# Second and third FFN: seven half-size products from the seventh unit on, and an adding transfer for the weights used last

## The chip, the cores and the metric

The kernel runs on one core of one Trainium2 chip. A core has TensorE (PE in the profile; its weight loads are shown apart as PEld), VectorE (DVE), ScalarE (ACT), GpSimd (POOL) and SyncE (SP), each with an instruction stream of its own, worked off in order, and 16 DMA engines that all queues share. The metric is the device time in microseconds of one execution; the median over several runs counts.

## The reference

The reference is a small diffusion transformer of two layers over 256 latent tokens and 256 context tokens, width 1024, in float32. Each layer has half an FFN, a mixer (attention in the first, an mLSTM in the second) and half an FFN again, each with a modulation by the condition `c` before and a normalised residual sum behind it. Cut to what matters here:

```python
def half_ffn(h, shift, scale, gate, w_in, w_out, g, b):
    xm = modulate(h, shift, scale)            # h * (1 + scale) + shift
    a, u = jnp.split(xm @ w_in, 2, axis=-1)   # 1024 -> 2 x 2816
    y = (jax.nn.silu(a) * u) @ w_out          # 2816 -> 1024
    return post_norm(h, 0.5 * gate * y, g, b)

# per layer i: mod_lat = silu(c) @ ada_w[i] + ada_b[i], cut into nine vectors (shift, scale, gate
# of three parts); mod_ctx likewise from c_ctx
# order: FFN (0,0), attention, FFN (0,1), FFN (1,0), mLSTM, FFN (1,1); the last for latents alone
```

The first three FFNs work on latents and context together, 512 tokens.

## The kernel before

**Numbers in two parts.** TensorE multiplies in a rounded 32-bit format (fp32r). To keep float32's accuracy every operand x is held as h (x rounded) and l = x - h, and every product is three matmuls, h·h, h·l, l·h (`mm3`, line 238). The parts are made by `split` (lines 222 and 227): a copy on ScalarE gives h, a subtraction on VectorE gives l. Activations lie as `xh` and `xl`, 128 partitions x 8 blocks x 512 tokens (the latents' 256 first, `LAT`, then the context's, `CTX`).

**Weights.** A chunk is 128 x 1024 floats, 512 KB. `raw` loads it from SyncE's queue (line 207) into one of `RAW` = 3 buffers; `pair` takes one of `WB` = 7 buffers for its h and l; `split` fills them.

**An FFN** (`ffn`) has 22 units of 128 hidden columns, in two halves of 11, since the hidden values of one half (`gt`) fit in memory: 11 units, then eight output products over those 11 (`unit_out`), twice. An ordinary unit (`unit_in`) takes two chunks and 16 blocks of weights, 48 matmuls of 512 columns, into two PSUM tiles, and `ffn_g` (lines 568, 569) forms silu(a)·u and splits it. The first four units of an FFN (`LEAD`) run on the latents first and on the context later, while the norm before them is still ending for the context. At the end of the second half the last four output products run by latents and context apart, with the steps of the next norm in between.

**The fast units.** In the second half of the second and third FFN, `fast_in` treats the unit's product as a 2 x 2 block product (two halves of the depth; latents and context; a and u) and forms it from seven half-size products instead of eight, after Strassen and Winograd: 84 matmuls of 256 columns. It needs sums of weight blocks, made on VectorE for each unit (`s1` to `s4`, line 615, into a tile of their own), and sums of activations, made once in `fast_sums` during the last output products of the first half: three new operands (`made`), and the lower context half of `xh`, `xl` overwritten. Line 650 is the unit's SiLU, lines 649, 653 and 654 its other VectorE steps.

**Modulation vectors.** They are made by VectorE: `ada_load` (line 331) brings 128 rows of the weight matrix, 512 KB, and `ada_dot` (line 337) multiplies them with the silu of c or c_ctx (`cb`) and sums, a dot. What layer 1 needs (40 loads for both vectors, 32 for one, 112 dots) is spread over the second and third FFN by the table `DOTS`: so many dots behind every unit (`in`) and output product (`out`). A load and its dots are written one directly behind the other; two buffers. `cb` is loaded and put through silu again (`silu_all`, line 306) whenever the memory has been used by the fast units.

**What sets the order.** The kernel is written on a tile framework: a planner at build time simulates the engines and issues, for each, what is ready by its own clock, earlier written first; buffers and waits follow from that. The chip then runs each stream in exactly that order. An instruction given to `pin` stays behind the one written before it on its engine: the dots, the norm's small steps and the residual steps (`residual`, lines 543 and 544: the old residual is scaled, two blocks behind every ordinary unit) are pinned. So a VectorE instruction that waits for a load holds up all behind it.

## Time and profile before

| | |
|---|---|
| median of 3 runs | 1652.38 us (1650.39 to 1652.40) |
| the profiled execution | 1649.32 us, span 1647.6 us |
| TensorE busy | 1617.8 us, 98% |
| VectorE busy | 1353.8 us, 82% |
| ScalarE busy | 744.2 us, 45% |
| read from memory | 249.81 MB, 152 GB/s over the span |
| mean granted TensorE clock | 0.993 |

The span goes from the first to the last instruction. By the times of the SiLUs, the second FFN runs from about 577 to 930 us of the span and the third to about 1300; the mLSTM follows to about 1457, the last FFN to the end. A line of a group reads: code line, engine, operation, output<-inputs, shapes, count | busy time, mean ns of one | idle time of the engine just before them and what ended it. A stage's line reads: from:to, length, then the busy time of PE, PEld, DVE, ACT and POOL with the number of instructions, the granted clock, the DMA engines' busy share and GB/s. Matmuls overlap in the engine, so the distance of their starts, not their length, says what one costs.

### The profile page before, as it was taken

How to read it: one execution, taken by the hardware profiler on the slowest of the kernel's cores; microseconds unless marked ns; L12 is line 12 of the kernel's file. 1: busy time of each engine (PE TensorE's matmuls, PEld its weight loads, DVE VectorE, ACT ScalarE, POOL GpSimd, SP SyncE). 2: the span in 40 equal slices, each digit the busy share in tenths (PEclk: the TensorE clock that was granted, in tenths of full speed). 3: DMA queues.
4: the chain of work that ended last, by engine and by line, in shares of the span. 5: the costliest groups of instructions: out<-in, count | busy, mean ns of one | idle time of the engine just before them, and what ended most of it. 6: DMA issues, size and time to landing. Idle time of an engine off the chain costs nothing. (4 is left out here: it accounts for less than half of the span.)

```text
span 1647.6 us, 26587 instructions
## 1 busy us (share of the span) xinstructions
PE 1617.8 (98%) x10308; PEld 1457.4 (88%) x10308; DVE 1353.8 (82%) x2689; ACT 744.2 (45%) x1269; POOL 61.6 (4%) x76
## 2 busy tenths in 40 slices
PE   9999999999999999999999999899999999999998
PEld 6888888899988998889999998689999989999987
DVE  5899978649888879999977977799965968897687
ACT  5532222314676343425652433225652656656542
POOL 0000000001011200000000100000000100020000
PEclk9999999999999999999999999899999999999999
DMA  9577765622103247733353267733352342437652
GB/s 371 187 237 231 239 215 187 203 76 84 65 1 91 64 143 229 229 128 129 103 182 126 78 193 255 250 120 116 115 155 66 116 120 78 135 109 256 181 172 96
DMA packets 72495, 252.59 MB, mean 153 GB/s; under 512 B 7984, under 2 KB 10800, under 8 KB 72368
## 3 DMA queue, kind: packets, MB, share of 16 engines
q1 hardware_dynamic: 71792, 250.10, 47.8%
q8 instruction: 81, 1.33, 0.3%
q10 hardware_dynamic: 576, 0.79, 0.1%
q14 instruction: 46, 0.38, 0.1%
HBM read 249.81 MB, written 1.05 MB: 152 GB/s over the span
## 5 line engine op out<-in xcount | busy, mean ns | idle before, releaser
L238 PE MATMUL t<-t,t 128*128 128x256 f32 (+2 forms) x8412 | 1325.1, 319 | 14.2 <-ACT t L222 10.7
L238 PEld LDWEIGHTS t<-t,t 128*128 128x128 f32 x8412 | 1193.1, 189 | 133.9 <-ACT t L222 12.7
L222 ACT CAST t<-t 128x1024 fp32r<-128x1024 f32 (+3 forms) x521 | 429.6, 844 | 467.3 <-PE t L238 244.3
L227 DVE TENSOR_TENSOR t<-t,t 128x256 fp32r<-128x256 f32 (+2 forms) x740 | 514.7, 728 | 116.6 <-ACT t L222 112.5
L337 DVE SCALAR_TENSOR_TENSOR t<-t,t 128x1024 bf16<-128x1024 f32 x224 | 263.5, 1220 | 25.2 <-DMA t<-in_ada_w 24.5
L909 PE MATMUL t<-t,t 128*128 128x256 f32 (+1 forms) x256 | 79.5, 311 | 0.0
L911 PE MATMUL t<-t,t 128*128 128x256 f32 (+1 forms) x256 | 78.8, 308 | 0.0
L910 PE MATMUL t<-t,t 128*128 128x256 f32 (+1 forms) x256 | 78.4, 306 | 0.0
L568 ACT ACTIVATE t<-t 128x512 f32<-128x512 f32 (+1 forms) x71 | 34.3, 487 | 95.6 <-PE t L238 95.6
L692 DVE SCALAR_TENSOR_TENSOR t<-t,t,t 128x256 f32<-128x256 f32 x96 | 42.7, 478 | 37.0 <-PE t L238 37.0
L569 DVE TENSOR_TENSOR t<-t,t 128x512 f32<-128x512 f32 (+1 forms) x71 | 38.9, 551 | 32.8 <-PE t L238 26.7
L464 POOL TENSOR_TENSOR t<-t,t 128x256 f32<-128x256 f32 x30 | 23.4, 781 | 1130.9 <-ACT t L454 1129.7
L1424 PE MATMUL t<-t,t 128*128 128x512 f32 (+3 forms) x286 | 60.2, 365 | 2.0 <-ACT t L1501 1.0
L837 PE MATMUL t<-t,t 128*128 128x512 f32 (+1 forms) x300 | 60.7, 364 | 0.0
L1424 PEld LDWEIGHTS t<-t,t 128*128 128x128 f32 (+2 forms) x286 | 43.8, 159 | 18.3 <-issue 2.2
L837 PEld LDWEIGHTS t<-t,t 128*128 128x128 f32 x300 | 51.4, 189 | 9.1 <-DVE t L831 0.3
L454 ACT ACTIVATE t<-t 128x256 f32<-128x256 f32 x72 | 26.2, 411 | 72.3 <-DVE t L447 72.3
L544 ACT ACTIVATE t<-t,t 128x256 f32<-128x256 f32 x64 | 29.4, 503 | 57.4 <-DVE t L543 57.4
L909 PEld LDWEIGHTS t<-t,t 128*128 128x128 f32 x256 | 48.4, 189 | 2.7
L910 PEld LDWEIGHTS t<-t,t 128*128 128x128 f32 x256 | 48.2, 188 | 2.6
L911 PEld LDWEIGHTS t<-t,t 128*128 128x128 f32 x256 | 48.1, 188 | 2.5
L615 DVE TENSOR_TENSOR t<-t,t 128x512 f32<-128x512 f32 x66 | 45.3, 686 | 1.1 <-DMA t<-in_ffn_in 0.3
(200 smaller groups left out, 1065.5 us busy)
## 6 DMA issues: line engine op xcount, KB each, us to landing
t<-in_ffn_in SPq DMA_DIRECT2D x168, 512.0 KB, 4.1
t<-in_ada_w SPq DMA_DIRECT2D x137, 512.0 KB, 4.2
t<-in_ffn_out SPq DMA_DIRECT2D x66, 512.0 KB, 4.4
t<-in_ffn_last SPq DMA_DIRECT2D x22, 512.0 KB, 3.5
t<-in_att_in SPq DMA_DIRECT2D x12, 512.0 KB, 3.5
t<-in_c SPq DMA_DIRECT2D x8, 512.0 KB, 7.8
t<-in_att_out SPq DMA_DIRECT2D x8, 512.0 KB, 3.5
t<-in_ml_qk SPq DMA_DIRECT2D x8, 512.0 KB, 3.6
```

Of the source, the lines that this page charges most:

```text
L222: self.behind(self.nc.scalar.copy(h, x))
L227: self.behind(self.nc.vector.tensor_tensor(out=ls, in0=xs, in1=hs.bitcast(F32), op=ALU.subtract))
L238: mm = lambda *k, **kw: self.nc.tensor.matmul(*k, skip_group_check=not group, **kw)
L337: ins = nc.vector.scalar_tensor_tensor(self.tmp().bitcast(BF16), r, 1.0, self.cb[:, v, :], ALU.mult, ALU.mult, accum_out=to)
L569: V.tensor_tensor(out=sl, in0=sl, in1=pu[:, :n], op=ALU.mult)
L615: add = lambda o, x, y: V.tensor_tensor(out=o, in0=x, in1=y, op=ALU.add)
L692: V.scalar_tensor_tensor(z, y[:, gg[0] - t0 : gg[1] - t0], gate()[:, v, d : d + 1], z, ALU.mult, ALU.add)
L837: pin(nc.tensor.matmul(o, gs[g], ws[k][w][:, i : i + n], start=k == k0 and g == w == 0, stop=k == k1 - 1 and g == 1,))
L909: mm(o, self.xh[:, k, c], wh, start=k == 0, stop=False)
L910: mm(o, self.xh[:, k, c], wl, start=False, stop=False)
L911: mm(o, self.xl[:, k, c], wh, start=False, stop=k == ND - 1)
L1424: mm = lambda *k, **kw: pin(nc.tensor.matmul(*k, **kw))
```

## The change

Three things are changed together, all for the second and third FFN, with what they need around them.

- From the seventh unit on (`FIRST` = 6) units are fast, in both halves: 16 of 22 for 11. So the sums of activations are made in the lead units: `fast_sums` behind the second lead unit's context part, in whole pieces of 1024 columns, and `fast_last`, which overwrites the lower context half, behind the last ordinary unit's matmuls. The buffers of `gt` for units 7 to 10 lend their room to these sums before they are needed (`gtiles`).
- In a fast unit the sums of weights are made in place in the two raw chunks, in another order, and the products come in the order a11, s1, s2, s4, s3, a12, a22. The pair of a12 and a22, used last, gets its parts by `split_added`: ScalarE writes h and -h, and a transfer from GpSimd's queue reads the chunk from memory a second time and adds it to -h.
- The dots: a load is issued at one call and its dots are made at a later one (`ada`, `flush`); `DOTS` names units one by one, and has places in the mLSTM too; counted through the loop `some`, the second FFN makes 46 dots, the third 47, the mLSTM 19 (there were 68, 44 and none). `cb` is loaded once and stays. One ada buffer while the fast units' operands are in memory and in the mLSTM.

Memory moves with it: a fourth raw buffer, five buffers for temporaries (a sixth where an FFN, the attention or the last FFN has room), the norm's sums in a pool of their own.

```diff
...
-RAW = 3
+RAW = 4
...
-SUMSAT = 4
+FIRST = 6
+GONE = 7
 FLIP = 56
 DOTS = {
-    1: {("in",): 4, ("out", 0): 3, ("out", 1): 2},
-    2: {("in",): 3, ("out", 0): 2, ("out", 1): 3},
+    1: {**{("in", j): 2 for j in (6, 8, 10, 12, 15, 18, 21)}, **{("out", 0, d): 2 for d in range(6)},
+        ("out", 0, 6): 4, ("out", 0, 7): 4, **{("out", 1, d): 2 for d in range(3)}, ("out", 1, 3): 4},
+    2: {**{("in", j): 2 for j in (6, 8, 10, 12, 15, 18, 21)}, **{("out", 0, d): 2 for d in range(6)},
+        ("out", 0, 6): 4, ("out", 0, 7): 4, **{("out", 1, d): 2 for d in range(3)}, ("out", 1, 3): 4},
+    "ml": {**{("key", n): 1 for n in range(5)}, **{("val", n): 1 for n in range(6)}, **{("unit", n): 1 for n in range(9)}, ("unit", 9): 2, ("unit", 10): 2},
 }
...
         self.fine = False
 
         self.nraw, self.spare = 0, None
+        self.ntmp, self.extra = 0, None
...
     def tmp(self, w=512):
-        return self.t([P, 512], tag="tmp", bufs=6)[:, :w]
+        self.ntmp += 1
+        if self.extra and self.ntmp % 6 == 0:
+            return self.t([P, 512], tag="tmpx", bufs=1, pool=self.extra)[:, :w]
+        return self.t([P, 512], tag="tmp", bufs=5)[:, :w]
...
+    def split_added(self, x, h, l, src=None):
+        self.nc.scalar.copy(h, x)
+        self.nc.scalar.activation(l, x, AF.Copy, scale=-1.0)
+        self.nc.gpsimd.dma_start(l, x if src is None else src, accum_op=ALU.add)
...
+        self.cb = self.t([P, 2, D])
+        self.waiting = []
+        self.norms(2)
+
...
+    def norms(self, n):
+        self.npool, self.np = self.right()
+        self.adas = self.np, n
...
-        r = self.t([P, 1024], tag="ada", bufs=2, pool=self.cp)
+        pool, n = self.adas
+        r = self.t([P, 1024], tag="ada", bufs=n, pool=pool)
...
     def ada(self, layer, dt, vecs=(0, 1)):
-        r = self.ada_load(layer, dt)
-        for v in vecs:
-            self.ada_dot(r, layer, dt, v)
+        self.waiting.append((self.ada_load(layer, dt), layer, dt, vecs))
+
+    def flush(self, n=0):
+
+        done = 0
+        while len(self.waiting) > n:
+            r, layer, dt, vecs = self.waiting.pop(0)
+            for v in vecs:
+                self.ada_dot(r, layer, dt, v)
+            done += len(vecs)
+        return done
...
+    def gtiles(self, j):
+        if j not in self.gt:
+            n, i = self.gw, j % NFH - GONE
+            if self.gn == NF or i < 0:
+                bufs = NF if self.gn == NF else GONE
+                self.gt[j] = tuple(self.t([P, n], F32R, tag=k, bufs=bufs, pool=self.gp) for k in ("gh", "gl"))
+            else:
+                assert i % 2 == 0
+                x = self.t([P, 4 * n], F32R, tag=f"g{i}", bufs=1, pool=self.gp)
+                for m in range(2):
+                    self.gt[j + m] = tuple(x[:, (2 * m + k) * n : (2 * m + k + 1) * n] for k in range(2))
+        return self.gt[j]
...
-    def fast_sums(self, i):
+        at = [i * n + (FLIP if i > 3 else 0) for i in range(6)]
+        self.slots = [x[:, a : a + n].rearrange("p (k f) -> p k f", f=TL) for a in at]
+        self.made = [self.slots[i : i + 2] for i in (0, 2, 4)]
+
+    def fast_sums(self):
 
...
+        lo, up = slice(0, ND // 2), slice(ND // 2, ND)
+        k = lambda x, i: x[:, i * 1024 : (i + 1) * 1024].rearrange("p (k f) -> p k f", f=TL)
+        x2, x1 = (self.t([P, 2048], tag=f"g{i}", bufs=1, pool=self.gp) for i in (0, 2))
+        t3, t2, t1, t4 = k(x2, 0), k(x2, 1), k(x1, 0), k(x1, 1)
+        add = lambda o, x, y, op=ALU.add: V.tensor_tensor(out=o, in0=x, in1=y, op=op)
+        less = lambda o, x, y: V.scalar_tensor_tensor(o, x, -1.0, y, ALU.mult, ALU.subtract)
+
+        def whole(o, ks, g):
+            add(o, self.xh[:, ks, g[0] : g[1]].bitcast(F32), self.xl[:, ks, g[0] : g[1]].bitcast(F32))
+
+        whole(t1, lo, LAT)
+        whole(t3, lo, CTX)
+        add(t1, t1, t3, ALU.subtract)
+        whole(t4, up, CTX)
+        add(t3, t4, t3, ALU.subtract)
+        less(t2, t1, t4)
+        whole(t4, up, LAT)
+        less(t4, t2, t4)
+        self.split(t3, *self.made[1])
+        self.split(t2, *self.made[0])
+        self.kept = t1, t4
+
+    def fast_last(self):
+
+        t1, t4 = self.kept
+        self.split(t1, *(x[:, : ND // 2, TL:T] for x in (self.xh, self.xl)))
+        self.split(t4, *self.made[2])
+
+    def fast_in(self, j, w_in):
...
         r0, r1 = (self.raw(w_in[2 * j + i]) for i in range(2))
-        sums = self.t([P, 4 * half], tag="sums", bufs=1, pool=st)
         part = lambda x, i: x[:, i * half : (i + 1) * half]
-        a11, a21, a12, a22 = part(r0, 0), part(r0, 1), part(r1, 0), part(r1, 1)
-        s1, s2, s4, s3 = (part(sums, i) for i in range(4))
-        add = lambda o, x, y: V.tensor_tensor(out=o, in0=x, in1=y, op=ALU.add)
-        ws = [self.pair(sh=SH, n=half)] + [self.pair(sh=SH) for _ in range(3)]
-        self.split(a11, *ws[0])
-        self.split(r1, *ws[1])
-        add(s1, a21, a22)
-        add(s2, s1, a11)
-        self.split(sums[:, : 2 * half], *ws[2])
-        add(s4, s2, a12)
-        add(s3, a11, a21)
-        self.split(sums[:, 2 * half :], *ws[3])
-        w = {n: [part(x, i) for x in ws[p]] for n, p, i in (
-            ("a11", 0, 0), ("a12", 1, 0), ("a22", 1, 1), ("s1", 2, 0), ("s2", 2, 1), ("s4", 3, 0), ("s3", 3, 1),
+        (a11, a21), (a12, a22) = ([part(r, i) for i in range(2)] for r in (r0, r1))
+        w1, w0, w2, w3 = self.pair(sh=SH), self.pair(sh=SH), self.pair(sh=SH, n=half), self.pair(sh=SH)
+        add = lambda o, x: V.tensor_tensor(out=o, in0=o, in1=x, op=ALU.add)
+        self.split_added(r1, *w1, w_in[2 * j + 1])
+        add(a22, a21)
+        add(a21, a11)
+        self.split(r0, *w0)
+        add(a11, a22)
+        add(a12, a11)
+        self.split(a11, *w2)
+        self.split(r1, *w3)
+        w = {n: [part(x, i) for x in p] for n, p, i in (
+            ("a11", w0, 0), ("s3", w0, 1), ("a12", w1, 0), ("a22", w1, 1), ("s2", w2, 0), ("s4", w3, 0), ("s1", w3, 1),
         )}
...
         a, u = self.tmp(), self.tmp()
         product(x, "a11", of(0, LAT), True, False)
         S.copy(a[:, :TL], x)
-        product(y, "a12", of(ND // 2, LAT), True, True)
         product(v, "s1", of(0, CTX), True, False)
         S.copy(u[:, TL:], v)
         product(x, "s2", made(0), False, False)
         S.copy(a[:, TL:], x)
+        product(v, "s4", of(ND // 2, CTX), False, True)
+        product(x, "s3", made(1), False, True)
+        product(y, "a12", of(ND // 2, LAT), True, True)
         product(z, "a22", made(2), True, True)
         S.copy(u[:, :TL], z)
-        product(v, "s4", of(ND // 2, CTX), False, True)
         V.tensor_tensor(out=a, in0=a, in1=yv, op=ALU.add)
         S.activation(a, a, AF.Silu)
-        product(x, "s3", made(1), False, True)
...
-    def ffn(self, layer, s, gate, groups, side, start=None, cpool=None):
+        self.split(a, *self.gtiles(j))
...
+            if not fast:
+                self.extra, self.adas = gp, (gp, 2)
...
+            def unit_in(j, w, g, steps={}, ks=range(ND), ps=None, late=None):
...
+                if late:
+                    late()
...
+                        if fast and j == first[1]:
+                            self.flush()
+                            self.npool.close()
+                            tpool, st = self.right()
+                            self.adas = st, 1
+                            self.fast_operands(st)
+                            self.fast_sums()
                     for j in first:
                         call("in", j)
                     js = js[LEAD:]
-                fast = cpool is not None and hf == 1
                 for j in js:
-                    if fast:
-                        self.fast_in(j, w_in, st)
-                        continue
-                    unit_in(j, stream(j), allg)
+                    if fast and j >= FIRST:
+                        self.fast_in(j, w_in)
+                    else:
+                        unit_in(j, stream(j), allg, late=self.fast_last if fast and j == FIRST - 1 else None)
...
+                if fast and hf:
+                    self.flush()
+                    tpool.close()
+                    self.norms(1 if layer else 2)
...
-                if fast:
-                    more.close()
-                    cpool = self.silu_all()
                 for d in range(body):
-                    if cpool and not hf and d == SUMSAT:
-                        cpool.close()
-                        self.n += 1
-                        more = ExitStack()
-                        st = more.enter_context(self.tc.tile_pool(name=f"st{self.n}", bufs=1, side="right"))
-                        self.fast_operands(st)
                     unit_out(hf, d, w, allg)
-                    if cpool and not hf and d >= SUMSAT and d - SUMSAT < 2:
-                        self.fast_sums(d - SUMSAT)
...
+                self.some(DOTS["ml"].get(("key", n - MH), 0))
...
+                self.some(DOTS["ml"].get(("val", n), 0))
...
+                self.some(DOTS["ml"].get(("unit", n), 0))
...
@@ -1600,35 +1643,40 @@
             for _ in range(3 if len(queue) > 40 else 2):
                 if queue:
                     b.ada(*queue.pop(0))
+                    b.flush(b.adas[1] - 1)
+            if not queue:
+                b.flush()
 
         def some(n):
-            while n > 0 and later:
-                n -= len(later[0][2])
-                b.ada(*later.pop(0))
-
+            while n > 0 and (later or b.waiting):
+                if b.waiting:
+                    n -= b.flush(len(b.waiting) - 1)
+                if later and len(b.waiting) < b.adas[1]:
+                    b.ada(*later.pop(0))
+
+        b.some = some
...
```

90 lines of the change are left out of this document (29 added, 61 removed).

## The prediction

> **What bounds the kernel now.** I read the profile's page first (busy shares, the 40 slices), then the instructions of one line in one stage (the pace of the two kinds of FFN unit), the groups of the fast units, the busy time by stage, and last the timeline where TensorE stands still.
>
> ```profile
> span 1647.6 us, 26587 instructions
> PE 1617.8 (98%) x10308; PEld 1457.4 (88%) x10308; DVE 1353.8 (82%) x2689; ACT 744.2 (45%) x1269; POOL 61.6 (4%) x76
> PE   9999999999999999999999999899999999999998
> DVE  5899978649888879999977977799965968897687
> ```
>
> TensorE is the bound nearly everywhere. VectorE is the next: 82% over the span, 90% or more in many slices. So a change is worth the TensorE time that it takes away, minus what VectorE, now asked for more, gives back. Only 29.8 us of the span are without a matmul. Each ordinary unit ends in one SiLU at line 568, each fast unit (the seven products) in one at line 650; the distance of two of them is the unit's time. First the ordinary units of the first FFN, then the fast ones of the third:
>
> ```profile
> L568 ACT ACTIVATE t<-t x11: 598/598/600, 213.3 to 322.1; 128x512 f32<-128x512 f32 x11
> L650 ACT ACTIVATE t<-t x10: 625/627/627, 1124.0 to 1211.6; 128x512 f32<-128x512 f32 x10
> 1133.60:1211.60 78.00, 78.00 (x675) 78.00 (x674) 70.86 (x93) 48.46 (x82) 0.00 (x0) 1.00 0.36 110
> ```
>
> An ordinary unit takes (322.1 - 213.3) / 10 = 10.88 us: 48 products of 512 columns at 0.2267 us. A fast unit takes (1211.6 - 1124.0) / 9 = 9.73 us: 84 products of 256 columns at 0.1159 us. The third line is a stage (length; PE, PEld, DVE, ACT, POOL busy; clock, DMA share, GB/s): in eight fast units TensorE never stops, VectorE is busy 70.86 / 8 = 8.86 us of each 9.73, the DMA engines 0.36 of the time.
>
> **The change part by part.**
>
> *1. Ten units become fast.* Units 6 to 10 of both FFNs: 10 x (10.88 - 9.73) = 11.5 us less TensorE. It is TensorE time, so it comes off the span if the new units are fed.
>
> *2. VectorE and ScalarE in a fast unit.* By group, in the same 78 us:
>
> ```profile
> L227 DVE TENSOR_TENSOR t<-t,t 128x1024 fp32r<-128x1024 f32 x25 | 30.6, 1223 | 6.9 <-ACT t L222 6.2
> L615 DVE TENSOR_TENSOR t<-t,t 128x512 f32<-128x512 f32 x21 | 14.4, 686 | 0.2
> L227 DVE TENSOR_TENSOR t<-t,t 128x512 fp32r<-128x512 f32 x15 | 10.3, 684 | 0.0
> L222 ACT CAST t<-t 128x1024 fp32r<-128x1024 f32 x26 | 27.4, 1052 | 13.2 <-PE t L238 13.2
> ```
>
> A fast unit makes three low parts of 1024 columns on VectorE (25 in eight units), afterwards two: the low part of a12 and a22 is -h on ScalarE plus a transfer that adds the source. So 8.86 - 1.22 = 7.6 us of VectorE, and one instruction of 1024 columns more on ScalarE (four for three): 48.46 / 8 = 6.1 us becomes 7.1, still under 9.73. Against an ordinary unit (two splits of 1.22, line 569 and a split of 0.68) a new fast unit asks VectorE for 7.6 - 3.8 = 3.8 us more.
>
> *3. The dots (products with the modulation weights, line 337).*
>
> ```profile
> L337 DVE SCALAR_TENSOR_TENSOR t<-t,t x60: 1211/1219/1227, 614.0 to 723.3; 128x1024 bf16<-128x1024 f32 x60
> L337 DVE DVE_READ_ACCUMULATOR t<-t,t x60: 76/81/89, 615.1 to 724.5; 128x1 f32 x60
> 613.00:698.00 85.00, 85.00 (x376) 70.40 (x375) 83.17 (x139) 29.65 (x43) 0.00 (x0) 1.00 0.75 229
> 698.00:745.00 47.00, 47.00 (x209) 38.94 (x208) 46.77 (x83) 10.82 (x14) 0.00 (x0) 1.00 0.37 121
> 1222.00:1245.00 23.00, 23.00 (x103) 19.03 (x103) 11.40 (x30) 7.17 (x8) 0.00 (x0) 1.00 0.48 161
> L543 DVE SCALAR_TENSOR_TENSOR t<-t,t,t 128x256 f32<-128x256 f32 x64 | 28.0, 476 | 0.0
> ```
>
> One costs VectorE 1.22 + 0.08 = 1.30 us. The second FFN's first half has 60 of them now and, by the table DOTS worked through its loop, 26 afterwards; VectorE is full there (130 of 132 us) without a stop of TensorE. 34 x 1.30 = 44 us go, 5 x 3.8 = 19 come: room. The tight stretch is units 6 to 10 alone: 5 x 7.6 + 6 x 1.30 + ten residual steps (line 543) of 0.48 + the late split (1.2) = 51.8 us of VectorE beside 48.7 us of TensorE. The excess is 3.1 us per FFN; weights lie in seven pair buffers, four for a unit, so much of it is made ahead in units 4 and 5. Between 0 and 3.1 I take 1.0: together +2. The second halves take 8 dots in eleven fast units (11 x 7.6 + 8 x 1.30 = 94 us of VectorE in 107) and some twelve at the output products, where the third FFN has VectorE free for 11.6 of 23 us: nothing.
>
> *4. The operands' sums* move from the first half's output products to the lead units: eight sums and four splits of 1024 columns, 12 x 1.22 = 14.6 us, for 24 instructions of 0.68 (16.4 us). They take the place of 16 dots (20.8 us) there: nothing. But the lower context operand can only be overwritten after unit 5's last product, and unit 6 wants it second: cast 1.05 and low part 1.22, 2.3 us, covered by the product before it, 12 x 0.1159 = 1.4 us. If the planner keeps the written order TensorE waits 0.9 us per FFN, if it takes another product first 0: I take 0.9, +1.8 in all.
>
> *5. The stop in the third FFN.* The dots of its first half, the timeline of VectorE and TensorE, then two stages:
>
> ```profile
> L337 DVE SCALAR_TENSOR_TENSOR t<-t,t x44: 1215/1224/1228, 969.4 to 1085.6; 128x1024 bf16<-128x1024 f32 x44
> 1042.81 1.22 DVE L337 SCALAR_TENSOR_TENSOR t<-t,t 128x1024 bf16<-128x1024 f32 x1 [2.75 <-DMA t<-in_ada_w]
> 1053.98 1.23 DVE L337 SCALAR_TENSOR_TENSOR t<-t,t 128x1024 bf16<-128x1024 f32 x1 [2.37 <-DMA t<-in_ada_w]
> 1055.93 0.68 DVE L569 TENSOR_TENSOR t<-t,t 128x512 f32<-128x512 f32 x1
> 1057.31 8.92 PE L238 MATMUL t<-t,t 128*128 128x512 f32 x27 [7.55 <-ACT t L222]
> 1049.60:1057.30 7.70, 0.16 (x1) 0.00 (x0) 4.65 (x9) 1.57 (x4) 0.00 (x0) 0.66 0.80 273
> 1057.30:1062.40 5.10, 5.09 (x11) 3.76 (x12) 4.89 (x8) 0.90 (x1) 0.00 (x0) 0.50 0.51 181
> ```
>
> VectorE works in order. A dot is queued right behind its own load, stands waiting for it (2.75, 2.37 us), and the last unit's gate product (line 569) stands behind the dot; TensorE needs that unit for its first output product and stops for 7.55 us, then runs 5.1 us at a clock of 0.50, 2.55 us lost: 10.1 us. The change calls for dots of a load that was issued at the call before (the list `waiting`), and has 26 dots in that half for the 44 of now. So I take the stop as gone: -10.1; if it stays, 0. What is late next there is VectorE's own work of part 3.
>
> *6. The mLSTM gets dots.* The table has 24 places for them there, but counted through the loop only 19 are left by then: 11 behind its key and value products, 8 behind units 0 to 7.
>
> ```profile
> 1308.00:1366.00 58.00, 57.43 (x284) 48.34 (x285) 37.97 (x58) 35.36 (x52) 0.00 (x0) 1.00 0.37 109
> 1366.00:1430.00 64.00, 63.32 (x484) 60.83 (x483) 55.62 (x170) 43.14 (x97) 3.65 (x8) 1.00 0.33 104
> 1430.00:1457.00 27.00, 26.39 (x216) 25.23 (x214) 25.68 (x63) 15.92 (x27) 4.98 (x6) 1.00 0.53 167
> ```
>
> In the first stage VectorE is idle 20.0 us: 11 x 1.30 = 14.3 fit. In the second it is idle 8.4 us and 8 dots are 10.4; behind it comes a stage with 1.3 us idle, so what is late stays late. Each dot is pinned behind the instruction before it, and TensorE, at 63.32 of 64 us, has no slack for what is queued behind. Not hidden are 10.4 - 8.4 = 2.0 us if every gap can be used, 10.4 if none can; below that 0, if TensorE has work ahead that doesn't wait for VectorE. I take 4, near the lower end, because the products of the o gate stand free to be drawn forward.
>
> *7. The adding transfers*, 32 of 512 KB, from POOL's queue, which has nothing else in this stage (0.00 above). The trace has no such transfer. Nearest row, the plain load of the same size:
>
> ```profile
> t<-in_ffn_in SPq DMA_DIRECT2D x168, 512.0 KB, 4.1
> t<-in_ada_w SPq DMA_DIRECT2D x137, 512.0 KB, 4.2
> ACT t L306 <- DMA t<-in_c: 10.9, 4, 4.7
> ```
>
> Its low part is wanted by the sixth product, 5/7 of a unit in, and its buffer is the first of the unit to be taken, more than one unit ahead: over 10 us, against 4.1 for a plain load, or 8.2 at twice that. Occupancy: two loads take 0.36 x 9.73 = 3.5 us of the engines per unit, 1.75 each; the third may take 6.2, 3.6 times a plain one, before the engines fill the unit. So 0 from this, with an open upper end (a rival). A gain is excluded beyond part 2's. The Trainium skill ("DMA: Bandwidth & Descriptors", "Anatomy of one DMA — SWDGE (gpsimd) path") gives 2.0 us plus bytes over 436 GB/s for a plain DMA of this path, 3.2 us as an estimate here, and the sum would be the same by it; no run here shows it.
>
> The silu vectors (line 306) stay in memory instead of being loaded three times more. The waits for them (10.9 us) were ScalarE's, idle half the time: 0. One more raw buffer and one temporary less where the fast units run: 0.
>
> *Sum:* -11.5 + 2 + 1.8 - 10.1 + 4 = -13.8 us. The profiled execution takes 1649.32 us (span 1647.6), 0.19% under the median of 1652.38; I set the difference against the median: 1638.6, said as 1639.
>
> **The rivals.** A difference of 0.2%, 3.3 us, is about what a measurement of this kernel can tell from none.
>
> *The stop stays or another like it comes* (an ada load with one buffer, waited for in VectorE's queue). For it: the loads keep the same queue, and at the output products the table asks for four dots at once, so the second pair meets a fresh load. Against: all others are a call behind. -13.8 + 10.1 = -3.7: 1649, at the edge of what can be told. 0.15, half of it faster.
>
> *The adding transfer binds* (the other side). A transfer that reads, adds and writes back may hold an engine several times as long. Place: the 32 fast units, pace 3.5 + A instead of 9.73. It decides from A = 6.7 us (32 x 0.43 eats the 13.8); at 7.0 us, four times a plain one, 32 x 0.77 = 24.6: 1663. For it: rows of plain loads say nothing of adding. Against: 0.64 of the engines' time is free. 0.14.
> The Trainium skill ("SBUF — State Buffer", "Who interferes with whom") adds a way to it: POOL writes the descriptors of its own transfers and is locked out while VectorE runs an instruction in a two-port mode; the same page gives two-input instructions no such mode, and nearly all of VectorE's here are those, so I leave it inside this rival; no run here shows it.
>
> *VectorE becomes the bound in the mLSTM.* If none of the 19 dots hides, 24.7 us instead of 4: +6.9, 1659; slower from 17 us on. Against: 20 us idle in the first stage. 0.08.
>
> *Everything hides*: part 6 at 0, the late split reordered, both excesses made ahead: -21.6, 1631. 0.07.
>
> **How the numbers follow.** Forecast 0.56, rivals 0.15, 0.14, 0.08, 0.07. Faster: 0.56 + 0.07 + 0.07 = 0.70. Same: 0.08. Slower: 0.14 + 0.08 = 0.22. The forecast's own range is part 6 from 0 to 10.4 with the stop gone, 1635 to 1645. The range of 8 in 10 goes from 1629 (all hides) to 1656, which takes in the staying stop and the mild end of the mLSTM rival and leaves out the binding transfer and the full price of the dots.
>
> **What would show it.** SiLUs at line 650 of the old numbering 32 times, units 6 to 10 at about 9.7 us: part 1. No gap of several us and no clock of 0.5 at the third FFN's first output product: part 5. An mLSTM stage longer by about 4 us with VectorE over 90% busy: part 6. A gap under 1 us, twice, after the first product of unit 6: part 4. The prediction is wrong if fast units run above 10.4 us, with TensorE waiting for a transfer from POOL's queue, or if the mLSTM grows by more than 17 us.

## The result and the profile after

The changed kernel takes 1681.05 us (median of 4 runs, 1678.5 to 1681.2); the kernel before took 1652.39 beside it. The ratio is 1.0173, 95% interval 1.0155 to 1.019: slower by 28.7 us, where 13.8 us less had been forecast. From the page of the changed kernel:

```profile
span 1679.3 us, 27581 instructions
PE 1621.6 (97%) x10668; PEld 1469.0 (87%) x10668; DVE 1373.1 (82%) x2713; ACT 795.4 (47%) x1346; POOL 93.1 (6%) x108
...
PE   9999999999989999999999999999997998999998
...
DVE  5889977749898988868888978779977778898687
...
t<-in_ada_w SPq DMA_DIRECT2D x137, 512.0 KB, 3.7
```

TensorE's busy time has not fallen, though ten units have half-size products, and it stands still more. Where, the stages show: the five new fast units of a first half, the eleven of a second half, the third FFN's first half from its fifth unit on, the stretch from the third FFN's last output stage to the first 512-wide product of the mLSTM, and the mLSTM up to the last FFN. First the kernel after, then the kernel before (the columns as in the prediction).

```profile
633.50:686.50 53.00, 49.81 (x421) 48.77 (x420) 44.42 (x65) 35.72 (x61) 2.64 (x3) 1.00 0.63 162
746.40:861.50 115.10, 110.43 (x925) 108.99 (x924) 99.36 (x143) 74.04 (x116) 7.91 (x9) 0.99 0.69 177
972.80:1107.90 135.10, 131.82 (x783) 116.72 (x781) 105.04 (x167) 63.33 (x96) 6.18 (x7) 1.00 0.61 163
994.60:1048.00 53.40, 50.12 (x421) 49.10 (x420) 43.66 (x64) 35.76 (x61) 2.66 (x3) 1.00 0.62 159
1107.90:1223.30 115.40, 110.96 (x926) 109.47 (x925) 99.14 (x143) 73.97 (x116) 7.91 (x9) 0.99 0.68 177
1223.30:1333.70 110.40, 99.13 (x670) 91.05 (x669) 83.21 (x210) 36.00 (x65) 9.60 (x12) 0.94 0.47 152
1333.70:1481.30 147.60, 137.53 (x864) 122.53 (x862) 123.00 (x306) 81.64 (x151) 6.21 (x8) 0.99 0.53 165
```

```profile
747.20:854.80 107.60, 107.45 (x926) 107.23 (x925) 98.76 (x130) 66.11 (x109) 0.00 (x0) 1.00 0.40 124
966.70:1113.00 146.30, 138.75 (x602) 114.09 (x601) 120.61 (x205) 43.77 (x64) 0.00 (x0) 0.97 0.64 210
1113.00:1220.30 107.30, 107.30 (x926) 107.30 (x925) 96.09 (x127) 65.69 (x108) 0.00 (x0) 1.00 0.40 119
1220.30:1316.20 95.90, 94.23 (x668) 87.59 (x667) 67.60 (x182) 39.68 (x67) 8.80 (x12) 1.00 0.33 107
1316.20:1449.00 132.80, 131.83 (x866) 120.20 (x865) 103.59 (x261) 81.83 (x151) 3.65 (x8) 1.00 0.40 122
```

- Five new fast units take 53.0 and 53.4 us, where five ordinary ones take 5 x 10.88 = 54.4 and 48.65 had been expected.
- The eleven fast units of the second halves, which were fast already, take 115.1 and 115.4 instead of 107.6 and 107.3: +15.6 us in all.
- From the third FFN's last output stage to the mLSTM: 110.4 instead of 95.9, +14.5. The mLSTM: 147.6 instead of 132.8, +14.8.
- Against that the stop in the third FFN is gone: its first half from the fifth unit on took 146.3 us and takes 135.1, the five new fast units among them.

Four views show what TensorE waits for. First VectorE and TensorE (timeline) at the beginning of the second FFN's second half:

```profile
746.26 1.23 DVE L352 SCALAR_TENSOR_TENSOR t<-t,t 128x1024 bf16<-128x1024 f32 x1 [1.31 <-DMA t<-in_ada_w]
752.21 1.23 DVE L352 SCALAR_TENSOR_TENSOR t<-t,t 128x1024 bf16<-128x1024 f32 x1 [2.18 <-DMA t<-in_ada_w]
758.22 1.23 DVE L352 SCALAR_TENSOR_TENSOR t<-t,t 128x1024 bf16<-128x1024 f32 x1 [3.63 <-DMA t<-in_ada_w]
759.37 1.22 DVE L352 SCALAR_TENSOR_TENSOR t<-t,t 128x1024 bf16<-128x1024 f32 x1
760.51 1.22 DVE L243 TENSOR_TENSOR t<-t,t 128x1024 fp32r<-128x1024 f32 x1
...
761.79 8.46 PE L254 MATMUL t<-t,t 128*128 128x256 f32 x58 [3.09 <-DVE t L243]
```

The dots (line 352 of the new numbering) come in pairs 6 us apart: with one buffer a load is issued when the dots before it are done. The low part that the second fast unit needs (760.51) stands behind them in VectorE's queue, and TensorE waits. The same in the third FFN's last output stage and behind it (the dots of the stretch as a group: count, ns, first and last start; then the idle time before them, us and times; below it TensorE's timeline):

```profile
L352 DVE SCALAR_TENSOR_TENSOR t<-t,t x13: 1218/1226/1228, 1226.8 to 1286.2; 128x1024 bf16<-128x1024 f32 x13
...
  DMA t<-in_ada_w: 14.3, 10
```

```profile
1291.28 2.93 PE L450 MATMUL t<-t,t 128*128 128x1 f32 x10 [3.72 <-DVE t L487]
1297.24 1.19 PE L450 MATMUL t<-t,t 128*128 128x256 f32 x2 [3.03 <-DVE t L513]
```

Thirteen dots, (1286.2 - 1226.8) / 12 = 4.95 us apart: a landing of 3.7 us and a dot of 1.3. The chain lasts until 1287 us, past the 512-wide output products and in among the norm's steps, for which TensorE waits. In the mLSTM the 19 dots of the change wait in the same way (there were none before):

```profile
L352 DVE SCALAR_TENSOR_TENSOR t<-t,t x19: 1212/1226/1229, 1349.3 to 1456.0; 128x1024 bf16<-128x1024 f32 x19
...
  DMA t<-in_ada_w: 14.9, 12
```

Last, a new fast unit of a first half (ScalarE, then TensorE):

```profile
651.60 0.91 ACT L567 ACTIVATE t<-t,t 128x256 f32<-128x256 f32 x2 [2.04 <-DVE t L566]
652.41 0.35 ACT L681 COPY t<-t 128x256 f32<-128x256 f32 x1
...
652.81 3.35 PE L254 MATMUL t<-t,t 128*128 128x256 f32 x27 [0.84 <-ACT t L681]
```

ScalarE copies an accumulator out (lines 677, 679, 681) between two products that add into it. In the new order only one product, 12 x 0.116 = 1.4 us, lies between the two; before, two did. Here the copy came late because it stood behind a residual step that waited for VectorE.

### The profile page after: what moved, and what is told of

It reads as the page before. It is cut to its first block, busy times and chain, and to the rows that moved or that the text cites. A ratio compares the mean times of both kernels' runs of the same rounds, so it can differ in the third digit from the quotient of the medians.

```text
span 1679.3 us, 27581 instructions
## 1 busy us (share of the span) xinstructions
PE 1621.6 (97%) x10668; PEld 1469.0 (87%) x10668; DVE 1373.1 (82%) x2713; ACT 795.4 (47%) x1346; POOL 93.1 (6%) x108
## 4 chain that ended last, share of the span: by engine, by line
PE 64%; DVE 17%; DMA 8%; ACT 7%; issue 3%; SPq 0%; DVEq 0%; ACTq 0%
PE t L254 51%; DMA t<-in_ada_w 6%; DVE t L243 5%; PE t L876 4%; PE t L1468 3%; DVE t L352 3%; ACT t L238 3%; DVE t L653 2%; PE t L948 1%; PE t L950 1%; PE t L949 1%; ACT t L233 1%; PE t L450 1%; ACT t L234 1%; DMA t<-in_ffn_out 1%
## 5 line engine op out<-in xcount | busy, mean ns | idle before, releaser
L254 PEld LDWEIGHTS t<-t,t 128*128 128x128 f32 x8772 | 1203.8, 189 | 131.3 <-DVE t L243 11.8
L238 ACT CAST t<-t 128x1024 fp32r<-128x1024 f32 (+2 forms) x501 | 409.5, 841 | 446.5 <-PE t L254 253.6
L243 DVE TENSOR_TENSOR t<-t,t 128x256 fp32r<-128x256 f32 (+3 forms) x720 | 493.0, 720 | 96.4 <-ACT t L238 95.8
L653 DVE TENSOR_TENSOR t<-t,t 128x512 f32<-128x512 f32 x96 | 66.2, 689 | 16.3 <-ACT t L234 14.1
L602 ACT ACTIVATE t<-t 128x256 f32<-128x256 f32 (+1 forms) x61 | 28.6, 474 | 101.4 <-PE t L254 96.5
L603 DVE TENSOR_TENSOR t<-t,t 128x256 f32<-128x256 f32 (+1 forms) x61 | 32.1, 530 | 34.9 <-PE t L254 26.8
L876 PEld LDWEIGHTS t<-t,t 128*128 128x128 f32 x300 | 51.5, 189 | 8.9
L235 POOL DMA_DIRECT2D t<-in_ffn_in x32 | 28.3, 885 | 508.1 <-ACT t L234 257.6
L544 ACT ACTIVATE t<-t,t 128x256 fp32r<-128x256 f32 x72 | 33.2, 504 | 43.6 <-DVE t L543 43.6
L949 PEld LDWEIGHTS t<-t,t 128*128 128x128 f32 x256 | 48.2, 188 | 3.4 <-DVE t L243 0.8
L948 PEld LDWEIGHTS t<-t,t 128*128 128x128 f32 x256 | 48.2, 188 | 3.0 <-ACT t L994 0.3
```

The lines of the kernel that those rows point to most:

```text
L238: self.behind(self.nc.scalar.copy(h, x))
L243: self.behind(self.nc.vector.tensor_tensor(out=ls, in0=xs, in1=hs.bitcast(F32), op=ALU.subtract))
L254: mm = lambda *k, **kw: self.nc.tensor.matmul(*k, skip_group_check=not group, **kw)
L544: S.activation(xh, x, AF.Identity, bias=e)
L653: add = lambda o, x: V.tensor_tensor(out=o, in0=o, in1=x, op=ALU.add)
L876: pin(nc.tensor.matmul(o, gs[g], ws[k][w][:, i : i + n], start=k == k0 and g == w == 0, stop=k == k1 - 1 and g == 1,))
```

## The experiments

All are measured against the kernel before on the same chip (1650.7 to 1652.9 us). The changed kernel was timed beside it once, so a difference between runs from different chips is good to about 2 us. In runs whose expectation says that values stand as zeros or come out wrong, only the time counts.

**The adding transfer, undone.**

```diff
-        self.split_added(r1, *w1, w_in[2 * j + 1])
+        self.split(r1, *w1)
```

> The changed kernel, but the low part of a12 and a22 is made by VectorE again (cast and subtraction) instead of by the adding transfer. Theory A (the new order of the seven products is what slows the fast unit: an accumulator has to be copied out by ScalarE between two products that are only one product, 1.4 us, apart): the fast units keep their 10.4 to 10.5 us in the second halves and the whole stays at 1680 or goes up by as much as VectorE's extra 1.22 us per unit can't hide, 1680 to 1695. Theory B (the adding transfer is late or blocks the others): the eleven fast units of a second half go from 115 us back to about 108, and with the ten of the first halves the whole falls by 20 us, to about 1660.

1702.46 us (ratio 1.0302, 1.0284 to 1.0321): 21.4 us slower than the change. The second halves take 121 and 120 us. Theory B falls: the transfer isn't the brake, it saves what VectorE would otherwise not get done.

**The order of the products, twice.** e2_order has a12 as the third product and a22 ahead of s3; e10_order has a22 as the third and a12 ahead of s3, by this edit:

```diff
+        product(z, "a22", made(2), True, True)
+        S.copy(u[:, :TL], z)
         product(x, "s2", made(0), False, False)
         S.copy(a[:, TL:], x)
         product(v, "s4", of(ND // 2, CTX), False, True)
-        product(x, "s3", made(1), False, True)
         product(y, "a12", of(ND // 2, LAT), True, True)
-        product(z, "a22", made(2), True, True)
-        S.copy(u[:, :TL], z)
+        product(x, "s3", made(1), False, True)
```

> The changed kernel, but the products run in the order a11, s1, a12, s2, s4, a22, s3: two products between the two uses of each accumulator, where the change has one. Theory A: the waits of TensorE for ScalarE's copies go (0.35 to 1.1 us each, and the 0.1 us steps), the eleven fast units of a second half take 108 to 110 us instead of 115, the whole falls by 10 to 20 us, to 1661 to 1671. Theory B: the low part of a12 is wanted two or three products earlier, so a late adding transfer is met sooner: the second halves take 115 us or more, and the whole is at 1681 or above.

> The changed kernel with the seven products in the order a11, s1, a22, s2, s4, a12, s3: two products between two uses of every accumulator, and none of a12 and s1 side by side in one tile. Theory A (a ScalarE copy with only one product of 1.4 us to cover it is what the new units wait for): the five units of a first half take 50.5 to 51.5 us instead of 53.2, the eleven of a second half 111 to 113 instead of 115.2, the whole 1673 to 1677. If TensorE then waits for POOL's transfer, the low part of a22 being wanted third instead of seventh, the halves get no shorter: 1681 or more (theory B). If neither, the waits come from the weights' casts behind VectorE: 1679 to 1681.

e2_order took 1681.97 us, e10_order 1679.46 (ratio 1.0165, 1.0146 to 1.0184). By the whole time alone theory A would fall; the stages tell more. In e2_order a12 begins its sum in the tile half beside s1's, which is still open, and its output comes out wrong, so only its time counts (five new fast units: 51.6 us). The Trainium skill ("PSUM — Partial Sum Buffer", "The four PSUM rules") says why: a product that begins a sum clears the written marks of the whole 2 KB bank, so s4 overwrites s1 instead of adding. No trace shows that. The stages of e10_order:

```profile
631.80:681.70 49.90, 49.15 (x422) 48.74 (x421) 43.74 (x64) 36.38 (x63) 2.64 (x3) 1.00 0.63 165
741.50:857.20 115.70, 111.11 (x926) 110.27 (x926) 97.18 (x141) 72.85 (x117) 7.89 (x9) 0.97 0.67 173
```

Five fast units take 49.9 us instead of 53.0, so theory A holds in the first halves, and more than expected; nor is the transfer late, though its low part is wanted as the third product. The second halves stay at 115.7 and 114.0: something else holds them. The 3 us won in each first half were lost again further on: the stretch before the mLSTM took 118.5 us instead of 110.4.

**The dots that come too late, left out.** The first two runs moved more than the dots; the third shows what.

> The changed kernel without the ten products with the modulation weights that it puts into the third FFN's last output stage (the last ten modulation values are left out and stand as zeros; the nineteen of the mLSTM stay). Theory C (there they have one buffer, so each waits for a load that can start only when the product before it is done, one per 4.9 us; thirteen of them last until 1287 us and hold up the norm in VectorE's queue): the stretch from the last output stage to the first 512-wide product of the mLSTM falls from 80 us towards the 66 of the kernel before, the whole to about 1667. Rival D (that stretch is longer for another reason, such as the moved pools or one temporary less): 1678 to 1681.

> The changed kernel without the nineteen products with the modulation weights in the mLSTM (the last nineteen modulation values are left out and stand as zeros; the ten of the third FFN's last output stage stay). Theory E (these products, each waiting in VectorE's queue, cost the mLSTM 13 us, nearly what all nineteen take without cover, 24.7, halved): the mLSTM falls from 169 to about 156 us, the whole to about 1668. Rival D (pools and buffers): 1678 to 1681. If the stretch before the mLSTM stays at 80 us while this one falls, the two are separate costs.

1681.53 and 1690.26 us, and theory C and E seemed to fall. But every product in them was slower, from the first FFN on. Their edit had moved something else:

```diff
+    for c in (6, 7, 8):
+        b.mod[1, c] = b.t([P, 2, ND])
```

> The changed kernel with nothing but a place moved: the three small tiles (64 bytes a partition each) of the last modulation values are set aside at the start, so that what is laid out behind them lies 192 bytes higher. The runs without the products of the third FFN's last output stage and without those of the mLSTM both had every product slower (512 columns 228.9 ns instead of 226.7, 256 columns 119.6 instead of 116) and 22 us more of TensorE in all, and both had these tiles placed so. Theory F (the place alone does it): 228.9 and 119.6 ns, 1700 to 1704 us. Rival G (something else in those kernels, such as the values left out): 226.7 and 116 ns, 1681.

1698.66 us: theory F. The three small tiles push the seven weight buffers from byte 64256 of a partition to 64448 (the raw chunks and the temporaries move along; the operands that stream and the FFN's hidden values stay where they were). How many products start in the same 200 us of the first FFN, before that and with it:

```profile
100.00:300.00 200.00, 200.00 (x884) 165.62 (x883) 174.88 (x284) 54.08 (x63) 0.00 (x0) 1.00 0.70 220
```

```profile
100.00:300.00 200.00, 200.00 (x875) 164.12 (x874) 172.89 (x280) 53.94 (x63) 0.00 (x0) 1.00 0.70 217
```

1% fewer, at a full clock. So the dots were left out again with every tile in its place: a column of the modulation vectors is set to zero, no load, no dot.

```diff
+        if self.skip:
+            for v in vecs:
+                self.nc.vector.memset(self.mod[layer, dt // ND][:, v, dt % ND : dt % ND + 1], 0.0)
+            self.waiting.append((None, layer, dt, vecs))
+            return
```

> The changed kernel without the ten products with the modulation weights in the third FFN's last output stage, this time with every tile where the changed kernel has it (ten of the modulation values are left out and stand as zeros). Theory C (one buffer there: one product per 4.9 us, each behind a fresh load, until 1287 us, in front of the norm): the stretch of 80 us falls by 12 to 14, the whole to 1667 to 1669; products of 512 columns stay at 226.7 ns. Rival D (moved pools): 1678 to 1681.

> The same without the nineteen products of the mLSTM too (29 modulation values left out, standing as zeros; every tile in its place). Theory C and E (the two stretches pay separately): 1681 - 14 - 13 = 1654. If the mLSTM's cost is not the products' but the buffers' and the pools', it stays with the run before it, at 1667. The fast units, the stall behind the first half's output stage and the missing stop of the third FFN are as in the changed kernel, so this is also the sum of parts 1 to 5 and 7 alone.

> The changed kernel without the eight products with the modulation weights behind the last two output columns of the first half, in the second and third FFN (those modulation values are left out and stand as zeros; every tile in its place). Theory (they have one buffer, so the last of them is reached in VectorE's queue 12 us after the output products are over, with the first low parts of the second half behind it): the stall of 3.4 us at the second unit of the second half and the 0.7 us before it go, twice; the eleven units take 111 us, the whole 1672 to 1674. Rival (the stall is the pipeline of the fast units filling up): 1680 to 1682.

e7_noout1: 1664.99 us, 16.1 less than the change, for 11 dots; its stretch before the mLSTM is back at 94.7. e9_noboth: 1650.98 (ratio 0.9991, 0.9982 to 1.0001), 14.0 less again, for 18 more; its mLSTM takes 132.9. e11_out0: 1666.17, 14.9 less than the change, for 16 dots (eight in each of the two FFNs); a second half of it:

```profile
744.90:853.40 108.50, 107.95 (x926) 107.36 (x925) 89.94 (x127) 73.64 (x116) 7.89 (x9) 1.00 0.65 170
```

So 45 of the 112 dots cost about 45 us, at three places that pay apart. The rival (fast units filling up) falls.

**Everything at once.** e13_all joins e9_noboth, e11_out0 and the order of e10_order.

> The changed kernel with everything that the runs so far name taken away at once: without the products with the modulation weights in the third FFN's last output stage, in the mLSTM and behind the last two output columns of the first halves (these modulation values are left out and stand as zeros), and with the seven products in the order a11, s1, a22, s2, s4, a12, s3. If the causes add up: 1651 (without the first two groups) - 8 - 5 = 1638, which is what had been forecast for the change. If the fast units keep a pace of 10.4 us for a reason not named yet: 1645 to 1651.

1628.50 us (ratio 0.9867, 0.9845 to 0.9888). Added up: 1681.05 - 16.1 - 14.0 - 14.9 = 1636.1, and the other 7.6 are left for the order. One first and one second half:

```profile
630.90:680.80 49.90, 49.13 (x421) 48.71 (x420) 43.73 (x64) 36.53 (x63) 2.63 (x3) 1.00 0.63 164
740.70:848.20 107.50, 107.40 (x926) 107.20 (x925) 89.20 (x125) 74.33 (x117) 7.89 (x9) 1.00 0.68 167
```

The second half has the pace of the kernel before again. The causes named so far account for the time.

**Work or waiting?** Two runs keep the dots where the change has them, from the third FFN's last output stage on, but let them read what lies in memory already: e14_still without the loads, e16_unread with them.

```diff
-        return r
+        return self.cb[:, 0, :] if self.still else r
```

> The changed kernel, but from the third FFN's last output stage on the products with the modulation weights read a vector that lies in memory already, with no load (29 modulation values come out wrong; the number, the place and the length of VectorE's instructions stay). Theory W (what costs there is standing in VectorE's queue behind a fresh load): both stretches fall as without the products, the whole to about 1652. Theory V (what costs is VectorE's own time, 29 x 1.30 = 38 us): both stay, 1676 to 1681. Half and half would show in the two stretches apart.

> The changed kernel, with every load of the modulation weights issued as in it, but from the third FFN's last output stage on the products read a vector that lies in memory already instead of the loaded rows (29 modulation values come out wrong). With neither loads nor waits the time was 1652.3. Theory W1 (the waiting of VectorE's queue is what costs): 1652 to 1655 with the loads' traffic back. Theory W2 (the loads themselves cost, by the DMA engines' time, 29 x 0.5 MB, or by their place in SyncE's queue ahead of other loads): back at 1670 to 1681.

1652.34 and 1655.74 us, against 1650.98 without the dots at all. The group of these dots in e14_still:

```profile
L355 DVE SCALAR_TENSOR_TENSOR t<-t x29: 1204/1219/1226, 1234.8 to 1420.7; 128x1024 bf16<-128x1024 f32 x29
...
  DMA t<-in_ada_w: 0.2, 1
```

Theory W holds: set against the kernel before on its own chip, the 29 dots of 1.3 us, 38 us of VectorE, cost 1 to 2 us, and their loads 3 to 4 more, where the change pays 30. The rest is VectorE standing in front of a load with others queued behind. e16_unread alone could leave a rival, since its loads no longer wait in SyncE's queue for a free buffer and so hold up no weights there. But in the changed kernel, from the third FFN's last output stage to the end of the mLSTM (1223 to 1482 us), the dots are the only instructions that the waits put down to a load (us, times, longest):

```profile
DVE t L352 <- DMA t<-in_ada_w: 29.2, 22, 2.4
```

**A second buffer.**

```diff
-RAW = 4
+RAW = 3
-                    self.norms(1 if layer else 2)
+                    self.norms(2)
```

> The changed kernel with two buffers for the loads of the modulation weights in the third FFN's last output stage and in the mLSTM instead of one; the room comes from the fourth raw weight buffer (three, as in the kernel before). It computes everything. If one buffer is the cause, a load is issued before the product with the load ahead of it, the two stretches fall from 110 and 148 us to about 96 and 134, and what is left over 1652 + 1 is the price of the raw buffer. If the products wait all the same, because a call comes too soon after the last: 1670 to 1681.

1717.66 us. The mLSTM falls from 147.6 to 137 us, and VectorE's waits for these loads in it from 14.9 to 4.5 us, so the single buffer is the cause there. The stretch before it falls only to 106.5: nine of its thirteen dots still wait for their load, 12.1 us in all. But the second halves take 138 and 140 us: the raw buffer given away costs them 47 us. A raw buffer and an ada buffer are 4 KB a partition each; that is what the change had traded.

**The plain split with the rest out of the way.** The edit of e1_plain on e13_all.

> The run of 1628.5 us, with the low part of a12 and a22 made by VectorE instead of by the adding transfer (it leaves out the same products and values, which stand as zeros). The prediction costed the change's two transfers apart from the products. If VectorE has room once those products are gone (7.6 + 1.2 of 9.76 us in a unit), the time stays at 1628 to 1631 and the adding transfer pays only for products in the fast units; if the fast units have no room (as in the run with the plain split, where they took 11.0 us), it rises by 5 to 20 us.

1648.24 us: 19.7 us more, even with 45 dots gone. In a second half TensorE waits for ScalarE's casts, in gaps of 2.3 and 1.8 us:

```profile
746.10:859.70 113.60, 109.56 (x926) 109.15 (x925) 98.77 (x134) 65.93 (x108) 0.00 (x0) 0.98 0.38 116
```

**The stop in the kernel before.** One run calls for a dot one call after its load, as the change does; the other has fewer dots per call.

```diff
-    2: {("in",): 3, ("out", 0): 2, ("out", 1): 3},
+    2: {("in",): 2, ("out", 0): 3, ("out", 1): 3},
```

> The kernel before with one part of the change alone: in the second and third FFN a product with the modulation weights is called for one call after its load (the list of loads waited for, two buffers as they were). Theory (the stop of 7.55 us and the 2.55 us of half clock in the third FFN come from such a product standing in VectorE's queue behind its own load): both gone, 1652.9 - 10.1 = 1643. Rival (the stop has another cause, or the wait moves to another instruction): 1650 to 1654.

> The kernel before with one row of its table changed: in the third FFN two products with the modulation weights behind a unit instead of three, three behind an output column instead of two; the rest fall to its last output stage. Calling for them one call later did not take the stop away. Theory (the third of a call needs a load that can start only when the first has freed one of the two buffers, and a lag of VectorE builds up over eleven units): with two per call no fresh load is met, the stop of 7.5 us and the half clock behind it go, 1641 to 1644, unless the products of the last output stage cost what they cost in the changed kernel, 1.2 us each: then 1650 or more.

e6_before_ahead: 1654.08 us (1.0013, 1.0003 to 1.0023). The stop is there, 7.1 us. e12_spread: 1643.62 (ratio 0.9952, 0.9937 to 0.9967); the third FFN's first half takes 136.0 us and TensorE never stops. What VectorE waited for before the dots between 960 and 1060 us (us, times), in the kernel before, in e6_before_ahead and in e12_spread:

```profile
  DMA t<-in_ada_w: 14.9, 14
```

```profile
  DMA t<-in_ada_w: 16.1, 17
```

```profile
  DMA t<-in_ada_w: 1.5, 3
```

With three one-vector dots per call and two buffers the third load can't be ahead, whenever its dot is called. With two per call the waits go. The ten dots that are left fall to the third FFN's last output stage, with two buffers there: VectorE waits 3.4 us for their loads, they are through at 1249 us, and the stretch to the mLSTM takes 95.6 us, against 95.9 with no dots in it. In the changed kernel, with one buffer, thirteen dots cost 14.5 us at this place. This kernel, one row of a table away from the one before, is the fastest here of all that leave nothing out.

**A kernel from the causes, nothing left out.** f1 has the order of e10_order and moves the 112 dots: 25 into the first FFN, none into the mLSTM.

> A whole kernel that computes everything: the changed one with the order of e10_order and with all 112 products with the modulation weights of the second layer outside the mLSTM: 25 in the first FFN's second half and last output stage, where VectorE is idle 25 of 110 and 16 of 30 us, eight loads with two buffers in the second FFN's last output stage, the rest one load per call, each called for one call later, none fresh at an output stage's end. If moving them costs nothing: 1628.5 to 1634. If the first FFN's units or the extra four per first half overload VectorE: 1636 to 1645. Above 1645 the places cost as much as in the mLSTM.

1649.18 us (0.9991, 0.9982 to 1.0). The second halves run at 108 us, the mLSTM at 132.9; but the first FFN now stops as the third had, and the first halves from the fifth unit on, with four calls more, take 136 us, where e13_all, which leaves dots out, takes 131.6. The end of the first FFN's second half:

```profile
329.00:358.00 29.00, 25.75 (x106) 20.49 (x105) 23.37 (x51) 5.76 (x6) 0.00 (x0) 0.94 0.79 261
```

So these places were not free either: what the fast units of the first halves win is about what the dots cost there. Whether other places, or more buffers without taking one from the weights, would do better was not tried.

## Why the prediction was wrong

- **Part 1, ten units at 9.73 us: -11.5.** Measured 54.4 - 53.0 and 54.4 - 53.4, -2.4; with the order of e10_order -9.1 (49.9 and 49.8). The step that failed took the pace of units with another order of products. The order was in the diff; that it halves the cover of a ScalarE copy was not worked out.
- **Part 2, VectorE 7.6 and ScalarE 7.1 us a unit.** Right: in e13_all (89.20 - 4 x 1.30) / 11 = 7.6 and 74.33 / 11 = 6.8 (four dots lie in that stretch).
- **Part 3, the dots: +2 for the tight stretch, nothing for second halves and output stages.** This is the step that failed most. It counted VectorE's free time and found room. The room was there: 29 dots without their loads cost 1 to 2 us. What wasn't counted is that one buffer makes load and dots one chain of 5 to 6 us, that a call for four dots runs the chain twice, and that a late dot stands in front of the next unit's low part. The eight dots at the end of each first half cost 14.9 us for both halves; the thirteen of the third FFN's last output stage, for which the sum had nothing, 14.5.
- **Part 4, sums moved: 0, and +1.8 for the late split.** No gap stands behind the first product of the seventh unit; the late split hid. Of the 1.2 us per half that e13_all has over 5 x 9.73 = 48.65, 0.8 us are gaps at later units.
- **Part 5, the stop: -10.1.** It is gone, -11.2 with the new units' -1.0 in it, as forecast. But of the two reasons given only the smaller number of dots was one: e6_before_ahead has the other alone, and keeps the stop; e12_spread has only fewer dots per call, and loses it.
- **Part 6, the mLSTM: +4, at most 10.4.** Measured +14.8. The upper bound was VectorE's own time for eight dots; the cost was waiting for loads (14.9 us of it, above), which VectorE's own time doesn't bound.
- **Part 7, the adding transfer: 0.** Right: no gap of TensorE is put down to POOL in the stages above. Its rival (1663) falls; without the transfer the kernel is about 20 us slower. The fast units did run above the 10.4 us that was to show the prediction wrong (53.0 / 5 = 10.6, 115.1 / 11 = 10.5), but with TensorE waiting for VectorE and ScalarE, not for the transfer. The Trainium skill ("SBUF — State Buffer", "Who interferes with whom") describes a lock-out of POOL; POOL's issues show no sign of it, each of the 32 takes 0.87 to 1.02 us.
- **The rivals.** "The stop stays or another like it comes" had the mechanism, one buffer, waited for in VectorE's queue, but looked for it at one place and at 10.1 us, with 0.15. It came at three, for 45. "VectorE becomes the bound in the mLSTM" had one of these places, but took VectorE's own time as the price. "Everything hides" (1631) is what e13_all shows, at the price of 45 dots left out. "All others are a call behind" was the false sentence: with one buffer a load can't be issued while the last one is still to be read.

In numbers: -2.4 and -10.2 (parts 1 and 5), +15.6 in the old fast units, +14.5 and +14.8 behind them are +32.3; the spans differ by 31.7.

## What to carry to other kernels

Before work is moved into an engine's idle time, work out the cycle of its buffer: landing plus use, times the uses, against the time between calls; with one buffer nothing is ahead, and a wait in an in-order queue costs what is behind it, not what the instruction takes. When the order of products changes, count for every accumulator that is read in between how many products cover the read. And when an experiment removes something, keep every tile where it was, or measure the move by itself.

## What the runs showed of the hardware

**Where the weights lie changes the pace of the products.** With the weights 192 bytes further up, products of 512 columns start 200 / 875 = 228.6 ns apart instead of 200 / 884 = 226.2 (the two lines above), and 338 products of 256 columns in the last FFN take 40.2 us instead of 38.0, at a granted clock of 1.00 in both. The whole takes 17.6 us longer (e5_place). Of what these products read only the weights had moved. Why was not found out, and only these two places were measured.

**The adding transfer costs the DMA engines 1.8 times a plain load from SyncE's queue.** From the transfers of the changed kernel in 760 to 850 us (queue, kind: packets, MB, share of 16 engines; then the issues with their time to landing):

```profile
q1 hardware_dynamic: 3024, 11.01, 41.0%
q0 software_dynamic: 1296, 4.72, 31.1%
...
t<-in_ffn_in SPq DMA_DIRECT2D x15, 512.0 KB, 4.8
t<-in_ffn_in POOLq DMA_DIRECT2D x8, 512.0 KB, 7.5
```

Nine transfers of 0.524 MB from POOL's queue took 0.311 x 90 / 9 = 3.1 us of the engines each, 21 plain ones 0.410 x 90 / 21 = 1.76. They land 7.5 us after the issue here, 7.0 over the whole kernel. The estimate of 3.2 us, worked out from the fit of the Trainium skill for that path ("DMA: Bandwidth & Descriptors", "Anatomy of one DMA — SWDGE (gpsimd) path"), doesn't fit them. How much of the difference is the adding, and how much the queue and the loads beside it, no run shows.
